# Ranking small steps a constant distance ahead of the text's count, in a two-layer hybrid decoder step

## The chip, the cores and the metric

The kernel runs on one core of one Trainium2 chip. The metric is the device time of one execution in microseconds (us). Three runs of the kernel before took 1163.38, 1163.99 and 1165.86 us; the median is 1163.99.

## The reference

One inference step of a decoder trunk with two layers, for a prompt of 1024 tokens and a sample group of 8 x 8 tokens, 1088 columns in all, with 1024 channels and shared weights. Cut to what matters here, layer 0 is

```
h    = rmsnorm(x) ; proj = h @ w_in                      # 1024 -> 33 tiles of 128 columns
y_a  = a_b * conv3(a_c * a_h) * silu(a_z)                # mixer A
r,k,v,wl,al = token_shift(...)                           # mixer B, RWKV-7, 8 heads of 64
decay = exp(-exp(w_log)) ; kk = normalised k*k_k ; a = sigmoid(...)
S_t  = S_(t-1)*decay_t + (S_(t-1) @ -kk_t) (kk_t*a_t)' + v_t k_t'    # one state per head
y_b  = (groupnorm(S_t r_t) + bonus) * silu(b_z)
x    = x + [y_a, y_b] @ w_out
```

Layer 1 does the same round a pooling mixer and a chunked gating mixer, which are plain dense work. The outputs are the two activations and the new states. All is in 32-bit floats.

## The kernel before

**Dense products.** The 1088 columns are three blocks: block 0 (b0) has the 64 sample columns and 256 of the prompt (320 in all), b1 and b2 have 384 of the prompt each. A product (`product`, L156 to L167) is one 128-wide tile of a projection for one block. Weights and activations are split into a high and a low part, so each of the 8 steps over k is three matmuls (L162, L163, L164), 24 in a product. The weight comes in two halves by DMA (L141); ScalarE makes the high part (L145), VectorE the low part (L146), with four buffers for each (`WB = 4`). The result lies in one of two PSUM buffers, `dn`, until it is evicted. Products form one queue: each is issued after the last matmul of the one before (`later`). Layer 0 has for each block 13 qkv products (`shifted`), 4 gate products (`in_proj_bz`) and 16 of mixer A, and then 8 of the output projection (`out_proj0`) for each block.

**The recurrence.** The state goes in chunks of 64 tokens, and a group is two chunks. Three kinds of small steps serve it, with small matmuls, and short operations on ScalarE (ACT), VectorE (DVE) and GpSimd (POOL):

- `rwkv_prep`, once a group: decays, keys and queries scaled into the tiles BK and AR (L549, L552, L555), the Gram matrices of the chunk (L567, evicted by L570 and written to DRAM by L577).
- `rwkv_inverse`, once a block: it loads the block's Gram matrices again (L611) and inverts their 32 x 32 triangles by 31 steps on DVE, each of two dependent operations (L622, L624), and writes the result to DRAM.
- `recur`, once a block: merges of the inverse (L651, L663), the chain of chunks (`rwkv_chunk`: L772, L774, L791, L793, L797, L807, L808), group norm and output (`group_norm`, `group_out`), and for b0 the sample tokens; between them the preparation of the next block's groups, each behind a finished group of the chain. The steps are traced in streams that may not be queued on PE ahead of given product halves (`marks`, two for each product); the recurrence of b0 and b1 starts 10 marks into the qkv products of the next block, that of b2 at the first product of `out_proj0(b0)`.

The blocks are coupled. The inputs of preparation (`s28`, `tw`, KS, R, V) have one buffer each, so b1's qkv tiles are written over b0's once preparation has read these. The last four input tiles of an output projection are what the recurrence wrote to DRAM (`yr`).

**What sets the order.** Tile queues are fixed when the program is built. A planner plays the program through with its own costs; whenever an engine is free, it takes, of the operations whose inputs it takes to be ready, the one of lowest rank. What isn't ready in that play is passed over. The rank is a running count: each operation traced takes the next number. `tc.high_priority()`, here also `urgent`, sets the count to zero inside its block, and puts it back at the end, so that the operations in the block don't count outside. With a number, the block starts at the count less that number; the result may be negative. Weight splits, evictions, whole qkv products and the recurrence all stand in such blocks, and a qkv product's matmuls have ranks 2 to 25. The count reaches 188 at the preparation of b0, 1361, 1902 and 2398 at the recurrences of b0, b1 and b2, and 5021 at the end. Inside a recurrence block it runs to about 800, and then through the next inverse. The preparation of the sample group and the inverse of b0 are not urgent: they rank by the text.

Of the kernel before, what the change touches and what calls it, by code (L numbers as in the profile page):

```python
# [17 lines left out]
NT = 1088  # L18
AT = (10, 10, 0)
EARLY, RATE, PREP_RATE = 20, 0.7, 0.5  # L20
BLK = ((0, 320), (320, 384), (704, 384))
KAPPA = float(np.exp(-0.5))
RMS_EPS, LN_EPS, GN_EPS = 1e-6, 1e-5, 64e-5
# [50 lines left out]
def build(nc, tc, a):  # L74
# [8 lines left out]
    def mk(p, shape, name, bufs=1, dt=F32):  # L83
        return p.tile(list(shape), dt, name=name, tag=name, bufs=bufs)
# [42 lines left out]
    G.memset(onesc, 1.0)  # L127

    urgent = tc.high_priority
    ydr = {}  # L130
    x1dr = {}

# [308 lines left out]
    def big4(name="iv"):  # L441
        return mk(rw, [128, 32, 32], name, 2)
# [7 lines left out]
    def rwkv_begin(B):  # L450
        n = B.n
        smp = B.i == 0
        s0 = 64 if smp else 0
        B.ng = (n - s0) // 128
        B.gl = ([(0, 64, None)] if smp else []) + [(s0 + 128 * g, 128, g) for g in range(B.ng)]
        B.i0 = 1 if smp else 0
        B.nch = 2 * B.ng + B.i0
        B.PC = mk(rw, [128, 6, 4], "PC", 2)
        B.GT, B.BK, B.AR, B.XT = {}, {}, {}, {}
        B.bon = mk(dr, [128, 4, 384], f"bn{B.i}")  # L460
        B.vd = mk(dr, [384, 512], f"vd{B.i}")
        B.yr = mk(dr, [128, 4, 384], f"yr{B.i}")
        B.dl = mk(dr, [B.nch, 8, 64, 64], f"dl{B.i}")
# [137 lines left out]
    def rwkv_inverse(B):  # L601


        nch, i0 = B.nch, B.i0
        n8 = nch * 8
        Q = 2 * n8
        Lb = big4()
        for (t0, T, g) in B.gl:
            lo, k = (0, 1) if g is None else (i0 + 2 * g, 2)
            for b in range(2):  # L610
                nc.gpsimd.dma_start(Lb[b * n8 + 8 * lo:b * n8 + 8 * (lo + k)],  # L611
                                    B.dl[lo:lo + k, :, 32 * b:32 * b + 32, 32 * b:32 * b + 32].rearrange(
                                        "i h s t -> (i h) s t"))
        X = big4()
        G.memset(X[:Q], 0.0)
        G.memset(X[:Q].rearrange("p a b -> p (a b)")[:, 0:1024:33], 1.0)
        prod = mk(rw, [128, 256], "prod")
        for q in range(31):
            k, r = q + 1, 31 - q
            o = X[:Q, 0:k, k:32]  # L620
            pr = prod[:Q, 0:k * r].rearrange("p (k r) -> p k r", k=k)
            tt(pr, X[:Q, 0:k, q:q + 1].broadcast_to([Q, k, r]),  # L622
               Lb[:Q, q:q + 1, k:32].broadcast_to([Q, k, r]), ALU.mult)
            tt(o, o, pr, ALU.add)  # L624
        for b in range(2):
            nc.gpsimd.dma_start(B.dl[:, :, 32 * b:32 * b + 32, 32 * b:32 * b + 32].rearrange("i h k t -> (i h) k t"),
                                X[b * n8:(b + 1) * n8])
        Xn = big4()
        V.tensor_copy(Xn[:n8], X[:n8].rearrange("p k i -> p i k"))
        B.dn = mk(dr, [nch, 8, 32, 32], f"dn{B.i}")  # L630
        nc.gpsimd.dma_start(B.dn.rearrange("i h k t -> (i h) k t"), Xn[:n8])
# [267 lines left out]
    def out_proj0(B, norms={}):  # L899

        n = B.n
        c0 = BLK[B.i][0]
        h = []
        for k in range(KT):
            x = mk(ev, [128, 384], *(("x", 6) if B.i == 0 else ("ma", 3)))
            nc.sync.dma_start(x[:, :n], ydr[(B.i, k)][:, :n])
            hi = mk(ring, [128, 384], "hi", RB, F32R)
            lo = mk(ring, [128, 384], "lo", RB, F32R)
            split_to(hi[:, :n], lo[:, :n], x[:, :n])
            h.append((hi, lo))  # L910
        acc = None
        for t in range(8):
            if t in norms:
                norm1(norms[t])
            w = weight(a["wout0"][t])
            ps = psum_d(n)
            product(ps, w, h, 0, n)
            if t == 0:
                late_rstd(pd, "dn")
            x = mk(ev, [128, 384], "x", 6)  # L920
            nc.sync.dma_start(x[:, :n], a["xT"][t, :, c0:c0 + n])
            with urgent():
                tt(x[:, :n], ps, x[:, :n], ALU.add)
                if t == 0:
                    acc = mk(cpool, [128, 384], "acc")
                    act(acc[:, :n], x[:, :n], AF.Square)
                else:
                    sq = mk(ev, [128, 384], "d", 1)
                    act(sq[:, :n], x[:, :n], AF.Square)
                    tt(acc[:, :n], acc[:, :n], sq[:, :n], ALU.add)  # L930
            xd = mk(dr, [128, 384], f"xd{B.i}_{t}")
            nc.sync.dma_start(xd[:, :n], x[:, :n])
            x1dr[(B.i, t)] = xd
        late.append((B, acc))
# [12 lines left out]
    for i in range(3):  # L947
        B = Blk()
        B.i, (B.c0, B.n) = i, BLK[i]
        Bs.append(B)  # L950
# [70 lines left out]
    b0, b1, b2 = Bs  # L1021
# [2 lines left out]
        V.tensor_scalar(kkbd[:, p, :], C("bd"), kk2[:, p:p + 1], None, ALU.mult)  # L1024
    rwkv_in(b0)
    rwkv_begin(b0)
    for x in b0.gl:
        with urgent() if x[2] is not None else ExitStack():
            for _ in rwkv_prep(b0, *x):
                pass  # L1030
    rwkv_inverse(b0)
    mark = tc.cur_priority
    rms_stat(b1)
    mixer_a(b0, hs[0], (0,))
# [10 lines left out]
    mixer_a(b1, hs[1], (1, 2))  # L1045
    rms_spread(b2)
    mixer_a(b1, hs[1], (3,))
    with urgent():
        recur(b0, at + AT[0], b1)
        rwkv_inverse(b1)  # L1050
    hs.append(rms_h(b2))
    at = len(marks)
    rwkv_in(b2)
    mixer_a(b2, hs[2], range(4))
    with urgent():
        recur(b1, at + AT[1], b2)
        rwkv_inverse(b2)
    at = len(marks)
    out_proj0(b0)
    out_proj0(b1)  # L1060
    with urgent():
        recur(b2, at + AT[2])
    nc.scalar.dma_start(a["shout"], shout)
    nc.scalar.dma_start(a["cvout"], cvout)
# [328 lines left out]
```

## Time and profile before

| | |
|---|---|
| median of three runs | 1163.99 us |
| profiled execution | 1167.19 us, span 1165.4 us |
| mean granted clock of TensorE over the span | 0.937 |
| PE, DVE, ACT, POOL busy | 1080.9, 741.9, 494.4, 155.9 us |

The profile is of one execution. PE is TensorE, DVE is VectorE, ACT is ScalarE, POOL is GpSimd, and SP issues most DMAs. L162 is line 162 of the kernel. A matmul's recorded duration covers its pipeline, so matmuls overlap in the records, and the step from one start to the next is what one costs. The granted clock is a share of 2.4 GHz.

### The profile page before, as it was taken

The page shows a single profiled execution, that of the slowest core. Times are in us where ns is not written, and L with a number is a line of the kernel's source. Part 1 is how long each engine was busy: PE and PEld are TensorE (multiplying, and loading weights), DVE is VectorE, ACT ScalarE, POOL GpSimd, SP SyncE. Part 2 cuts the span into 40 slices and gives each one's busy share as a digit, 9 for nine tenths or more (in the row PEclk, how much of TensorE's full clock was granted, in tenths as well). Part 3 has the DMA queues.
Part 4 walks back from the last instruction along what each step waited for, and adds up shares of the span by engine and source line. Part 5 has one row for each costly group of instructions (what it writes and reads, how often), then busy time and mean ns, then how long its engine had stood idle before and what let it go on. Part 6 is the DMA issues. An engine that isn't in the chain of part 4 may idle for free. (4 is left out here: it accounts for less than half of the span.)

```text
span 1165.4 us, 21579 instructions
## 1 busy us (share of the span) xinstructions
PE 1080.9 (93%) x8063; PEld 1018.0 (87%) x8063; DVE 741.9 (64%) x1542; ACT 494.4 (42%) x1017; POOL 155.9 (13%) x282
## 2 busy tenths in 40 slices
PE   7999999999998699999979887499999999999996
PEld 6998899898788598988869886399999999999995
DVE  6878885692788766938888743387383344235456
ACT  5376553434655533366654353254311211124232
POOL 2313220201202411102330010000010000000000
PEclk9999999998999799999979886679999999999998
DMA  7464663635345434444468653267311111112345
GB/s 248 154 207 131 160 194 128 200 132 125 99 148 174 123 106 141 139 117 131 133 179 248 211 142 102 58 207 233 109 41 37 39 60 39 37 55 82 111 150 187
DMA packets 135336, 154.83 MB, mean 133 GB/s; under 512 B 45560, under 2 KB 88696, under 8 KB 135232
## 3 DMA queue, kind: packets, MB, share of 16 engines
q1 hardware_dynamic: 130912, 146.36, 41.2%
q0 software_dynamic: 2256, 5.03, 2.1%
q10 hardware_dynamic: 2064, 2.08, 0.6%
q8 instruction: 63, 1.03, 0.4%
q14 instruction: 41, 0.34, 0.1%
HBM read 127.77 MB, written 25.64 MB: 132 GB/s over the span
## 5 line engine op out<-in xcount | busy, mean ns | idle before, releaser
L162 PE MATMUL dn<-hi,whi 128*128 128x384 f32 (+1 forms) x1648 | 553.1, 336 | 28.2 <-ACT q L320 10.6
L163 PE MATMUL dn<-lo,whi 128*128 128x384 f32 (+1 forms) x1648 | 549.6, 333 | 2.9 <-DVE lo L171 2.8
L164 PE MATMUL dn<-hi,wlo 128*128 128x384 f32 (+1 forms) x1648 | 547.2, 332 | 0.0
L162 PEld LDWEIGHTS dn<-hi,whi 128*128 128x128 f32 x1648 | 315.3, 191 | 34.0 <-ACT q L320 11.6
L145 ACT CAST whi<-wraw 128x512 fp32r<-128x512 f32 x326 | 201.4, 619 | 329.6 <-PE dn L163 282.0
L146 DVE TENSOR_TENSOR wlo<-wraw,whi 128x512 fp32r<-128x512 f32 x326 | 223.9, 688 | 161.0 <-ACT whi L145 154.6
L163 PEld LDWEIGHTS dn<-lo,whi 128*128 128x128 f32 x1648 | 315.3, 191 | 8.4 <-DVE lo L171 5.8
L164 PEld LDWEIGHTS dn<-hi,wlo 128*128 128x128 f32 x1648 | 315.2, 191 | 1.5 <-DVE wlo L146 0.5
L807 DVE TENSOR_TENSOR pch<-pch,SV 64x256 f32<-64x256 f32 x32 | 13.9, 434 | 40.6 <-PE pch L797 39.9
L183 POOL TENSOR_TENSOR rms_m<-rms_m,nhalf 128x3 f32<-128x3 f32 (+2 forms) x8 | 6.8, 852 | 216.5 <-DVE rms_m L182 216.5
L567 PE MATMUL pp<-AR,BK 64*128 64x128 f32 x272 | 28.0, 325 | 6.6 <-DVE BK L549 6.6
L567 PEld LDWEIGHTS pp<-AR,BK 64*128 64x128 f32 x272 | 25.3, 226 | 9.2 <-DVE BK L549 5.3
L624 DVE TENSOR_TENSOR iv<-iv,prod 80x31 f32<-80x31 f32 (+23 forms) x93 | 31.2, 336 | 2.1
L622 DVE TENSOR_TENSOR prod<-iv 80x31 f32<-80x31 f32 (+23 forms) x93 | 31.2, 336 | 2.0
L1284 DVE TENSOR_TENSOR big<-dn,x1s 128x384 f32<-128x384 f32 (+1 forms) x24 | 12.8, 535 | 27.6 <-PE dn L164 27.6
L723 POOL TENSOR_TENSOR gvs<-gvs,nhalf 128x8 f32<-128x8 f32 (+1 forms) x9 | 15.8, 1756 | 98.3 <-DVE gvs L722 98.3
L577 POOL DMA_DIRECT2D dl<-GT x32 | 20.2, 634 | 63.8 <-DVE GT L570 62.7
L1290 ACT ACTIVATE sq<-big 128x384 f32<-128x384 f32 (+1 forms) x21 | 10.7, 510 | 35.1 <-DVE big L1284 35.0
L403 POOL COPY pcarry<-up 128x2 f32<-128x2 f32 x12 | 6.4, 530 | 142.2 <-DVE up L394 110.7
L570 DVE TENSOR_TENSOR GT<-pp,cst 128x512 f32<-128x512 f32 x34 | 22.1, 686 | 3.6 <-PE pp L567 3.4
L743 PEld LDWEIGHTS pp<-cst,yc 64*64 64x64 f32 x256 | 12.1, 176 | 13.5 <-DVE yc L724 10.7
L743 PE MATMUL pp<-cst,yc 64*64 64x64 f32 x256 | 14.3, 270 | 10.0 <-DVE yc L724 10.0
(282 smaller groups left out, 1291.4 us busy)
## 6 DMA issues: line engine op xcount, KB each, us to landing
wraw<-win SPq DMA_DIRECT2D x246, 256.0 KB, 2.6
wraw<-wout SPq DMA_DIRECT2D x80, 256.0 KB, 3.2
x<-xT SPq DMA_DIRECT2D x48, 192.0 KB, 3.5
xd<-x SPq DMA_DIRECT2D x16, 192.0 KB, 3.1
xn<-xd SPq DMA_DIRECT2D x16, 192.0 KB, 3.5
x1s<-xd SPq DMA_DIRECT2D x16, 192.0 KB, 2.4
yT<-big SPq DMA_DIRECT2D x16, 192.0 KB, 2.7
i<-vd SPq DMA_DIRECT2D x34, 64.0 KB, 3.4
```

What stands on the lines that cost most here:

```text
L145: A.copy(hi, raw)
L146: tt(lo, raw, hi.bitcast(F32), ALU.subtract)
L162: mm(ps, wh[:, k % 4, :], hh[:, c0:c0 + n], start=k == 0, stop=False)
L163: mm(ps, wh[:, k % 4, :], hl[:, c0:c0 + n], start=False, stop=False)
L164: i = mm(ps, wl[:, k % 4, :], hh[:, c0:c0 + n], start=False, stop=k == KT - 1)
L567: mm(gp[e][:, p * 128:(p + 1) * 128], BK[r, p, c, :, :].rearrange("p a s -> p (a s)"), AR[r, p, c, :, :].rearrange("p a s -> p (a s)"), st ...
L570: tt(GT[:, e::2, :], v3(gp[e]), m[e].unsqueeze(1).broadcast_to([128, 4, 128]), ALU.mult)
L577: nc.gpsimd.dma_start(of_half(B.dl[i], e), GT[64 * e:64 * e + 64, e::2, 0:64])
L622: tt(pr, X[:Q, 0:k, q:q + 1].broadcast_to([Q, k, r]), Lb[:Q, q:q + 1, k:32].broadcast_to([Q, k, r]), ALU.mult)
L624: tt(o, o, pr, ALU.add)
L723: G.tensor_tensor(vs[:T], vs[:T], nhalf[:T], ALU.pow)
L743: mm(ft[r, q:q + 64], yc[r, j:j + 64], ident[r, r], start=True, stop=True)
```

## The change

Four blocks get ranks by `tc.high_priority(6000)`, where they had ranks from zero on, or, for the preparation of b0's sample group and the inverse of b0, by the text. The instructions are the same.

```diff
+AHEAD = 6000
...
     urgent = tc.high_priority
+
+    def ahead():
+
+        return tc.high_priority(AHEAD)
...
     rwkv_begin(b0)
-    for x in b0.gl:
-        with urgent() if x[2] is not None else ExitStack():
+    with ahead():
+        for x in b0.gl:
             for _ in rwkv_prep(b0, *x):
                 pass
-    rwkv_inverse(b0)
+        rwkv_inverse(b0)
...
-    with urgent():
+    with ahead():
         recur(b0, at + AT[0], b1)
         rwkv_inverse(b1)
...
-    with urgent():
+    with ahead():
         recur(b1, at + AT[1], b2)
         rwkv_inverse(b2)
...
-    with urgent():
+    with ahead():
         recur(b2, at + AT[2])
```

## Rows read from the trace of the kernel before

**Rows 1.** The page: busy us of each engine, share of the span, instructions.
```profile
PE 1080.9 (93%) x8063; PEld 1018.0 (87%) x8063; DVE 741.9 (64%) x1542; ACT 494.4 (42%) x1017; POOL 155.9 (13%) x282
```
**Rows 2.** Stretches: from:to length, busy us of PE PEld DVE ACT POOL (instructions), clock, DMA.
```profile
151.00:206.00 55.00, 54.09 (x313) 53.77 (x313) 35.66 (x64) 22.80 (x43) 7.10 (x21) 1.00 0.49 155
206.00:262.00 56.00, 51.10 (x330) 49.49 (x329) 45.92 (x108) 22.69 (x48) 8.50 (x16) 0.97 0.54 167
...
368.00:407.00 39.00, 25.35 (x192) 21.06 (x190) 27.59 (x55) 18.57 (x45) 15.93 (x21) 0.79 0.48 130
...
504.00:588.00 84.00, 83.21 (x1095) 69.05 (x1094) 58.41 (x119) 57.32 (x133) 18.44 (x26) 1.00 0.45 125
588.00:611.00 23.00, 15.20 (x117) 12.34 (x115) 19.04 (x40) 10.91 (x23) 6.77 (x8) 0.70 0.54 159
...
636.00:681.00 45.00, 39.42 (x200) 37.22 (x199) 34.72 (x82) 17.29 (x32) 4.52 (x5) 0.89 0.68 206
681.00:763.00 82.00, 56.28 (x830) 47.21 (x828) 30.52 (x64) 32.46 (x81) 4.93 (x3) 0.63 0.35 93
```
**Rows 3.** PE in order of time, 680 to 757: start, us, instruction, count, wait before.
```profile
680.34 0.34 PE L162 MATMUL dn<-hi,whi 128*128 128x384 f32 x1
...
682.77 0.34 PE L164 MATMUL dn<-hi,wlo 128*128 128x384 f32 x1
...
738.42 0.69 PE L797 MATMUL pch<-i 128*64 128x64 f32 x16
...
756.76 0.69 PE L162 MATMUL dn<-hi,whi 128*128 128x384 f32 x1 [4.38 <-ACT hi L170]
```
**Rows 4.** The same stretches, L162 alone (one third of the dense matmuls).
```profile
151.00:206.00 55.00, 34.99 (x104) 19.39 (x105) 1.00 0.49 155
206.00:262.00 56.00, 26.93 (x77) 14.98 (x77) 0.97 0.54 167
...
368.00:407.00 39.00, 3.10 (x10) 1.67 (x9) 0.79 0.48 130
...
504.00:588.00 84.00, 20.10 (x57) 10.52 (x56) 1.00 0.45 125
588.00:611.00 23.00, 2.73 (x9) 1.65 (x8) 0.70 0.54 159
...
636.00:681.00 45.00, 23.29 (x65) 12.97 (x64) 0.89 0.68 206
681.00:763.00 82.00, 3.62 (x8) 1.76 (x7) 0.63 0.35 93
```
**Rows 5.** DVE in order of time: last BK write of block 0.
```profile
160.79 0.69 DVE L549 TENSOR_TENSOR BK<-tm,iP 64x512 f32<-64x512 f32 x1
```
**Rows 6.** PE in order of time: the Gram matmuls of that group.
```profile
206.76 2.06 PE L567 MATMUL pp<-AR,BK 64*128 64x128 f32 x32
```
**Rows 7.** PE and DVE in order of time: block 0's fourth chunk.
```profile
330.85 0.69 PE L797 MATMUL pch<-i 128*64 128x64 f32 x16
...
358.93 0.42 DVE L807 TENSOR_TENSOR pch<-pch,SV 64x256 f32<-64x256 f32 x1
```
**Rows 8.** DVE in order of time: first qkv tile of block 2.
```profile
395.98 0.62 DVE L339 SCALAR_TENSOR_TENSOR s<-d,pv,q 128x384 f32<-128x384 f32 x1 [0.84 <-PE pp L489]
```
**Rows 9.** DVE groups of the inverses (count, busy, mean ns, idle before); block 2's, timed.
```profile
L624 DVE TENSOR_TENSOR iv<-iv,prod 80x31 f32<-80x31 f32 (+23 forms) x93 | 31.2, 336 | 2.1
L622 DVE TENSOR_TENSOR prod<-iv 80x31 f32<-80x31 f32 (+23 forms) x93 | 31.2, 336 | 2.0
...
638.25 0.55 DVE L171 TENSOR_TENSOR lo<-ma,hi 128x384 fp32r<-128x384 f32 x1
638.72 0.41 DVE L622 TENSOR_TENSOR prod<-iv 96x252 f32<-96x252 f32 x1
```
**Rows 10.** The stretch in which one preparation group ran alone, all engines.
```profile
375.00:394.00 19.00, 12.84 (x95) 10.76 (x95) 13.12 (x27) 9.50 (x22) 6.44 (x11) 0.68 0.48 114
```
**Rows 11.** Waits of SP's queue: us in total, times, longest.
```profile
SPq L674 <- PE py L799: 32.6, 11, 7.5
```

## Prediction

> **What bounds the kernel now.** I read the page first, then the table of stretches, then single lines in time. On the page TensorE (PE) is busy 93% of the span [rows 1], so in the main a product waits for the product before it, and only stretches in which PE is idle, runs at a low granted clock, or runs small steps alone can give anything back. The table of stretches [rows 2] shows where these are: 206 to 262, 368 to 407, 588 to 611, 636 to 681 and 681 to 763. From 504 to 588, where small steps of the recurrence lie between the products, PE is busy 83.21 of 84 us at a granted clock of 1.00.
>
> Two prices come from here. A dense matmul of 384 columns costs PE 0.174 us at full clock: 14 steps of the same sequence from 680.34 to 682.77 [rows 3]; a product has 24, so 4.17 us. A small matmul between products costs 0.059 us: in 504 to 588 there are 1095 instructions [rows 2], 3 x 57 = 171 of them dense [rows 4] (each k has one of L162, L163 and L164), so 84 - 171 x 0.174 = 54.2 us for 924.
>
> What holds the small steps back is seen in three places.
>
> *Behind products of equal rank.* In 151 to 206 PE ran 313 instructions [rows 2], 3 x 104 = 312 of them dense [rows 4]: no small step. Yet the last DVE write of a group's BK was done at 161.48 [rows 5], and the Gram matmuls that read it began at 206.76, all 32 in a row [rows 6]. They had waited 45 us for nothing but their rank. The qkv products stand in an `urgent` block that restarts at zero, so their matmuls rank 2 to 25; the group's Gram step is about the fiftieth of its own block.
>
> *Behind evictions on DVE.* The fourth chunk's state product was on PE from 330.85 to 331.54; the DVE add that reads it ran at 358.93 [rows 7], 27 us late, in a queue filled with work of `urgent` blocks.
>
> *The other way round.* At 395.98 DVE could write the first qkv tile of block 2 (`s28`, one buffer) only when L489 of the last preparation group of block 1 had read it [rows 8]. So late preparation stops the products: that is the hole from 368 to 407.
>
> At the end of this chain stands the exposed tail. The last dense matmul of its run starts at 682.77, the next at 756.76 [rows 3]; between them the whole recurrence of block 2 runs alone, at a granted clock of 0.63 over the stretch [rows 2], a mix of the two levels, 2.4 and 1.2 GHz, while PE idled for 26 of its 82 us.
>
> **The change part by part.** No instruction is added or removed, no wait and no DMA. Four blocks get other ranks: preparation and inverse of block 0 start at 188 - 6000, the recurrence blocks at 1361, 1902 and 2398 less 6000. The text's count ends at 5021, so all four rank ahead of each `urgent` block, which starts at 0, where before their first instructions shared its ranks and the rest came after it.
>
> (a) *b0 preparation and inverse ahead.* The Gram step moves from 206.8 to about 162; the inverse and the first merge follow it, and the recurrence of block 0 starts some 30 to 45 us earlier (30 if the inverse takes longer beside the qkv products). The stretch 206 to 262 has 330 instructions, 231 dense: 40.2 + 99 x 0.059 = 46.0 us of PE work in 56. Gain 10.0 us.
>
> (b) *recurrence of b0 and preparation of b1 ahead.* The hole goes, as preparation is over before block 2's products ask for the buffer. 368 to 407: 192 instructions, 30 dense: 5.2 + 162 x 0.059 = 14.8 us in 39. Gain 24.2 us. Late next is the mark after which the recurrence of block 1 may be queued: 10 marks, so five products, into block 2's qkv, where no chunk of it ran in the trace.
>
> (c) *recurrence of b1, preparation of b2.* 588 to 611: 117 instructions, 27 of them dense, with 320 columns (27 x 0.174 x 320/384 = 3.9), plus 90 x 0.059 = 5.3: 9.2 in 23. Gain 13.8 us.
>
> (d) *recurrence of b2.* It may be queued from the first product of block 0's output projection on. If it starts there, its PE steps lie between the 16 products of two projections. 681 to 763: 830 instructions, 24 dense: 4.2 + 806 x 0.059 = 51.8 in 82. Gain 30.2 us. What stays is the tail behind the last chunk, group norm, output and a round trip through DRAM: 738.42 to 756.76, 18.3 us [rows 3]. It is hidden if the recurrence ends 18 us before the second projection does, bare if not: 0 to 18.3, and I keep 10, about the middle, as six chunks and 16 products are nearly equally long here.
>
> (e) *What pays: evictions and weight splits behind.* On DVE the 62 steps of an inverse take 0.336 us each [rows 9], 20.8 us together, and a preparation group about 13.1 [rows 10]. Dense work bears a DVE delay of two products, 8.4 us, as there are two PSUM buffers and four half-weight buffers. If such a block held DVE whole, an inverse would cost 20.8 - 8.4 = 12.4 us of PE and a group 4.7. But DVE had 55 - 35.66 = 19.3 us free in 151 to 206 [rows 2], and between dependent inverse steps it ran splits that rank far behind them (the L171 at 638.25, rank above 1902, before the L622 at 638.72, rank about 900) [rows 9]. So the bounds are 0 and 3 x 12.4 + 7 x 4.7 = 70 us (three inverses, seven groups that move among products); I take 3 us per inverse, 9 in all, near the lower end because of that row.
>
> (f) *Queues moved past.* On SP the recurrence's loads now go ahead of weight loads. Its chunk loads waited 32.6 us over 11 waits, the longest 7.5 [rows 11]; two products' worth of weights (8.4 us) hide each, and without that cover the price is at most 32.6. I take 0. On POOL the mask stores and inverse loads pass the little carry copies of the qkv tiles; two q buffers hide these.
>
> Sum: 10.0 + 24.2 + 13.8 + 30.2 - 10 - 9 = 59.2 us. The profiled execution took 1167.19 us (span 1165.4), so 1108; the median of the runs is 3.2 lower, so **1105 us**. 636 to 681 has 200 instructions, 195 dense: 33.9 + 0.3 in 45, another 10.8 us which I don't count, as its stall waits for loads that stay.
>
> A rule that speaks against (d): the row shows 924 small matmuls between products at a granted clock of 1.00 [rows 2]. The Trainium skill (Perfetto Trace Analysis, Matmul Optimizations) says that TensorE scales its power with utilization and that matmuls should therefore be issued back to back in batches. If interleaving brought the projections to the 0.63 of the tail, their products, 8 x 4.17 and, with 320 columns, 8 x 3.48 = 61 us, would take 61 x (1/0.63 - 1) = 36 us more, and the time would be about 1141. The trace disagrees, so it gets a chance of 0.04.
>
> **The rivals.**
>
> *PE-bound throughout.* The tail is fully hidden and DVE costs nothing: 78.2 us, 1086, or with the loads of 636 to 681 relieved too 1075. For it: the recurrence moves by more than the stall is long. Against: new order, new waits.
>
> *Only the front.* (a) and (b) come, but the inverse of block 2 stays as slow among the evictions as before and the recurrence still ends behind the projections: 34.2 - 9 = 25, 1139. For it: that inverse's steps already run at 638 [rows 9], over 100 us before dense work resumes, and chunk steps are latencies that rank doesn't shorten.
>
> *Nothing moves.* The order is that of the data and of the marks, 1164. Against it are [rows 5 to 7], where data was there and rank alone held.
>
> *Slower.* DVE becomes the bound where the blocks go: each of ten blocks is planned without gaps, evictions and splits come behind it, PE starves. Price: 70 us, and after each stall a product at the granted clock of 0.63, 4.17 x 0.59 = 2.5 us, so 25 more: 95, against 78.2 - 10 = 68 won; 1191. It decides once a block costs PE more than 68/10 = 6.8 us. For it: 206 to 262 has DVE busy 45.92 of 56 us, and inverses would now meet qkv products. Against: the L171 row.
>
> That the change doesn't do what it says is possible in one respect: block 1's recurrence starts at -4098, while block 0's ends near -3760, so ranks overlap; data keeps the order there, and it costs nothing.
>
> **How the numbers follow.** Forecast 0.50 (1086 to 1125), PE-bound 0.14, front only 0.12, cold clock 0.04, no change 0.06, slower 0.14. The range 1074 to 1150 holds the first four, 0.80. Faster by over 0.2% (2.3 us, about what a measurement of this kernel can tell from no change) 0.80, within it 0.06, slower 0.14.
>
> **What would show it.** (a) The Gram matmuls of block 0's last group run among the first qkv products, not behind the thirteenth. (b) The fourth chunk's L807 follows its L797 within some us, and block 2's first `s28` write waits for no L489. (c) First chunk of block 1 before 450. (d) No stretch of 74 us without dense matmuls; PE idle in the middle falls. (e) Single DVE gaps for evictions between inverse steps; if PE waits on L146 splits in runs of over 7 us during inverses, the slower rival is at work. A recurrence of block 2 that still starts after the second projection would make the forecast wrong.

## Result and profile after

The kernel after takes 1116.83 us (median of 4 runs, 1114.5 to 1121.83), the kernel before beside it 1163.68 (1158.56 to 1165.86). The ratio is 0.9609, with a 95% interval of 0.956 to 0.9658: faster by 47 us. The prediction was 1105, range 1074 to 1150. All code of the change's kernel lies five lines lower than before, so L167 of after is L162 of before, L572 is L567, L812 is L807. The program's instructions are the same, but ACT runs 6 fewer, all of them loads of activation tables (14 where it had 20).

The page of after, busy us of each engine, against [rows 1]:

```profile
PE 1049.7 (94%) x8063; PEld 991.6 (89%) x8063; DVE 735.2 (66%) x1542; ACT 485.3 (44%) x1011; POOL 159.9 (14%) x282
```

The 8063 PE instructions are the same, and yet PE is busy 31.2 us less; its idle time falls from 1165.4 - 1080.9 = 84.5 to 1112.7 - 1049.7 = 63.0 us. These 31.2 + 21.5 are the 52.7 us of the span. The busy part goes with the clock: the mean granted clock is 0.972, where it was 0.937.

Where it went is read from stretches between the same events: start, block 0's first mixer-A product, block 1's first qkv product, block 2's first qkv product, b0's first output product, b2's second output product. Columns as in [rows 2]. Before:

```profile
0.00:75.90 75.90, 67.47 (x442) 65.71 (x442) 58.51 (x130) 39.90 (x76) 17.77 (x59) 0.98 0.66 207
75.90:151.40 75.50, 72.61 (x515) 69.04 (x514) 63.96 (x142) 50.55 (x105) 21.10 (x34) 0.98 0.54 155
151.40:351.70 200.30, 193.71 (x1506) 175.32 (x1505) 135.94 (x274) 93.83 (x197) 25.65 (x49) 0.97 0.48 145
351.70:588.30 236.60, 220.10 (x1936) 200.44 (x1936) 173.34 (x355) 121.80 (x262) 55.28 (x84) 0.95 0.47 135
588.30:764.00 175.70, 136.60 (x1315) 122.40 (x1314) 105.76 (x237) 73.40 (x157) 16.01 (x16) 0.75 0.53 154
```

After:

```profile
0.00:97.50 97.50, 83.99 (x557) 78.17 (x558) 72.47 (x170) 51.83 (x109) 24.60 (x73) 0.96 0.52 164
97.50:184.20 86.70, 75.11 (x506) 71.26 (x505) 74.42 (x183) 42.17 (x89) 26.21 (x31) 0.94 0.58 163
184.20:396.90 212.70, 199.90 (x1601) 181.15 (x1601) 161.35 (x330) 104.61 (x219) 40.58 (x67) 0.96 0.50 148
396.90:604.50 207.60, 199.99 (x1807) 184.54 (x1806) 150.33 (x311) 109.27 (x231) 41.56 (x66) 0.97 0.50 143
604.50:709.90 105.40, 100.83 (x1240) 92.45 (x1239) 70.00 (x138) 62.48 (x138) 7.46 (x5) 1.00 0.73 222
```

The stretches change by +21.6, +11.2, +12.4, -29.0 and -70.3 us; what lies behind them is 401.4 us before and 402.8 after. So the front is **45.2 us longer** and the back **99.3 shorter**. Some of it is only moved: up to block 2's first qkv product PE runs 557 + 506 + 1601 = 2664 instructions where it ran 2463, nearly all of the difference small steps; at 0.059 us each about 12 us of work. That leaves a loss of some 33 us in front and a gain of some 87 behind.

**The front.** The longest stall of PE in the second stretch, from the list of waits (us in total, times, longest):

```profile
PE dn L184 <- DVE acc L284: 7.0, 1, 7.0
```

The matmuls on both sides of it, PE in order of time:

```profile
119.01 0.31 PE L169 MATMUL dn<-hi,wlo 128*128 128x320 f32 x1
126.35 1.44 PE L184 MATMUL dn<-onesc,acc 128*128 128x1 f32 x6 [7.04 <-DVE acc L284]
```

L284 sums the squares of block 1's input for its norm and ranks by the text; the product queue stands until the last of these sums. The input had landed by 78.0 us, and before, the last sum was done at 74. The last squares stand on ACT behind weight splits (L150) that wait for their loads, ACT in order of time:

```profile
119.04 0.62 ACT L150 CAST whi<-wraw 128x512 fp32r<-128x512 f32 x1 [2.02 <-DMA wraw<-win]
120.44 0.62 ACT L150 CAST whi<-wraw 128x512 fp32r<-128x512 f32 x1 [0.78 <-DMA wraw<-win]
120.96 0.52 ACT L283 ACTIVATE d<-x 128x384 f32<-128x384 f32 x1
123.34 0.62 ACT L150 CAST whi<-wraw 128x512 fp32r<-128x512 f32 x1 [1.86 <-DMA wraw<-win]
123.86 0.52 ACT L283 ACTIVATE d<-x 128x384 f32<-128x384 f32 x1
```

So rank left the sums until late, and weight loads that came late held the last of them. The clock falls within the stall and stays low behind it, as these two stretches show (columns as above):

```profile
118.00:126.00 8.00, 1.31 (x9) 1.05 (x8) 4.47 (x9) 3.23 (x6) 0.16 (x1) 0.77 0.92 268
126.00:130.00 4.00, 3.65 (x15) 3.65 (x16) 1.81 (x9) 0.00 (x0) 0.88 (x1) 0.50 0.60 203
```

Two more waits of PE in the front are of small steps ranked ahead, whose own input isn't there yet when PE's queue comes to them:

```profile
PE pp L572 <- DVE BK L554: 8.5, 3, 5.0
PE pp L601 <- DVE V L344: 5.6, 2, 5.4
```

Before, the first of these came to 1.1 us in the front and the second doesn't stand there.

**The small steps.** Single lines in order of time, which answer to [rows 5 to 8]: block 0's last BK write and its Gram matmuls, the fourth chunk's state product and its add, block 2's first qkv tile:

```profile
106.73 0.69 DVE L554 TENSOR_TENSOR BK<-tm,iP 64x512 f32<-64x512 f32 x1
106.24 3.28 PE L572 MATMUL pp<-AR,BK 64*128 64x128 f32 x32 [0.47 <-DVE BK L554]
...
265.70 0.69 PE L802 MATMUL pch<-i 128*64 128x64 f32 x16
276.14 0.42 DVE L812 TENSOR_TENSOR pch<-pch,SV 64x256 f32<-64x256 f32 x1
...
404.76 0.61 DVE L344 SCALAR_TENSOR_TENSOR s<-d,pv,q 128x384 f32<-128x384 f32 x1
```

The Gram matmuls follow their input at once, where they had waited 45 us. The add is still 10 us late, where it was 27. The qkv tile waits for nothing.

**The tail.** PE in order of time: the last chunk's state product (738.42 in [rows 3]), the last group output, and the output projection that needs it:

```profile
672.85 0.69 PE L802 MATMUL pch<-i 128*64 128x64 f32 x16
...
682.46 1.15 PE L748 MATMUL pp<-cst,yc 64*64 64x64 f32 x32
...
706.25 0.44 PE L167 MATMUL dn<-hi,whi 128*128 128x384 f32 x1 [1.11 <-ACT hi L175]
```

The recurrence of block 2 now begins at 610.2, where it was 686.9, and its 832 small steps lie among the products of 604.5 to 709.9 at a clock of 1.00.

### The profile page after: what moved, and what is told of

Read it like the earlier page. It is cut to its first block, busy times and chain, and to the rows that moved or that the text cites. A ratio compares the mean times of both kernels' runs of the same rounds, so it can differ in the third digit from the quotient of the medians.

```text
span 1112.7 us, 21507 instructions
## 1 busy us (share of the span) xinstructions
PE 1049.7 (94%) x8063; PEld 991.6 (89%) x8063; DVE 735.2 (66%) x1542; ACT 485.3 (44%) x1011; POOL 159.9 (14%) x282
## 4 chain that ended last, share of the span: by engine, by line
PE 75%; DVE 12%; DMA 5%; ACT 3%; issue 2%; POOL 1%; SPq 0%; DVEq 0%; ACTq 0%
PE dn L167 21%; PE dn L168 20%; PE dn L169 20%; DVE wlo L151 2%; DMA wraw<-win 2%; PE pp L572 1%; DMA xn<-xd 1%; DVE BK L554 1%; ACT whi L150 1%; PE pch L777 1%; PE pl L1182 1%; PE pl L1247 1%; PE pch L796 1%; DVE GT L575 1%; DVE prod L627 1%
## 5 line engine op out<-in xcount | busy, mean ns | idle before, releaser
L167 PE MATMUL dn<-hi,whi 128*128 128x384 f32 (+1 forms) x1648 | 554.3, 336 | 12.3 <-ACT whi L150 7.1
L150 ACT CAST whi<-wraw 128x512 fp32r<-128x512 f32 x326 | 200.2, 619 | 318.9 <-PE dn L168 277.5
L167 PEld LDWEIGHTS dn<-hi,whi 128*128 128x128 f32 x1648 | 313.6, 190 | 20.7 <-ACT whi L150 9.3
L572 PE MATMUL pp<-AR,BK 64*128 64x128 f32 x272 | 28.5, 317 | 9.5 <-DVE BK L554 8.5
L572 PEld LDWEIGHTS pp<-AR,BK 64*128 64x128 f32 x272 | 25.5, 216 | 12.9 <-issue 6.9
L331 DVE TENSOR_TENSOR d<-q 128x384 f32<-128x384 f32 (+1 forms) x39 | 20.7, 530 | 6.0 <-ACT q L325 4.5
L1203 ACT ACTIVATE big<-dn 128x384 f32<-128x384 f32 (+1 forms) x12 | 5.7, 472 | 35.0 <-PE dn L169 35.0
L928 DVE TENSOR_TENSOR x<-dn,x 128x384 f32<-128x384 f32 (+1 forms) x24 | 12.8, 532 | 10.6 <-PE dn L169 6.9
```

The costliest lines, as they stand in the source:

```text
L150: A.copy(hi, raw)
L167: mm(ps, wh[:, k % 4, :], hh[:, c0:c0 + n], start=k == 0, stop=False)
L331: tt(d[:, :n], q[:, 0:n], q[:, 1:1 + n], ALU.subtract)
L572: mm(gp[e][:, p * 128:(p + 1) * 128], BK[r, p, c, :, :].rearrange("p a s -> p (a s)"), AR[r, p, c, :, :].rearrange("p a s -> p (a s)"), st ...
```

## Experiments

Times are medians; ratios are formed from the single runs against the kernel before on the same chip, with 95% intervals, so they differ a little from quotients of medians. Its medians there were 1165.28 us (7 runs) beside the first four kernels, 1163.35 beside the next four, 1165.36 beside the last four.

**Is it the order among the blocks, or being ahead at all?** e3 lets each block start at -6000:

```diff
-        return tc.high_priority(AHEAD)
+        return tc.high_priority(tc.cur_priority + AHEAD)
```

> The changed kernel, but each of the four blocks starts at the same rank, -6000, instead of a constant distance ahead of the text. If what counts is that the blocks rank ahead of the urgent products and evictions, the time is that of the changed kernel, within 0.5%. If what counts is that the blocks keep their order among themselves, most of the gain is lost: 1140 to 1165 us.

1119.07 us, 0.9599 (0.9568 to 0.963). PE's queue is the change's own. That the blocks keep their order among each other does nothing; that they rank ahead of the `urgent` blocks does.

**Each part alone.** e1 is the change with block 0's part put back; e2 has that part alone.

```diff
 # e1
-    with ahead():
-        for x in b0.gl:
+    for x in b0.gl:
+        with urgent() if x[2] is not None else ExitStack():
...
-        rwkv_inverse(b0)
+    rwkv_inverse(b0)
```

> The changed kernel with one part undone: preparation and inverse of block 0 rank as before; the three recurrence blocks stay 6000 ahead. Theory A (the chain of the recurrence sets the end, and block 0's early start buys about what it costs on VectorE): the first merge is near 280 us again instead of 207, the front up to block 2's first qkv product is 20 to 35 us shorter than in the changed kernel (there 397), but the recurrence of block 2 starts well after block 0's output projection, so that the second projection's end is followed by a stall; 1105 to 1130 us against 1117. Theory B (block 0's part is cost alone, as the recurrence of block 1 waited for its mark in any case): the front is shorter and nothing is given back, 1085 to 1095.

> The kernel before with one part alone: only preparation and inverse of block 0 rank 6000 ahead; the recurrence blocks start at zero as before. Theory A: block 0's recurrence starts early (first merge near 207 us), but the preparation of block 1 still waits behind qkv products of equal rank, and the tail of block 2 stays exposed: 1150 to 1185 us, so little of the gain of 47. Theory B: cost alone, 1185 to 1200.

e1: 1121.82 us, 0.9596 (0.9538 to 0.9654; its longest run, 1130.83, is left out of the ratio), the same as the change. Its first stretches are 149.1 us long, not 184.2, but the next one takes up 28 of these 35 us, so block 2's first qkv product comes 7 us earlier where 20 to 35 were expected (columns as above; start to b1's first qkv product, and on to b2's):

```profile
0.00:149.10 149.10, 136.93 (x955) 132.09 (x956) 122.34 (x272) 90.27 (x179) 38.05 (x93) 1.00 0.61 184
149.10:389.90 240.80, 219.96 (x1706) 196.10 (x1706) 172.13 (x350) 110.78 (x241) 44.37 (x74) 0.94 0.49 139
```

e2: 1136.07 us, 0.9753 (0.9718 to 0.9789), a larger gain than expected. Its hole is gone too. Its theory A, by which block 1's preparation would still wait, fell. The parts don't add: each alone brings that preparation forward.

e9 has the block of b0's recurrence with b1's preparation and inverse alone ahead, e10 the two later blocks alone:

```diff
 # e9, the kernel before with
-    with urgent():
+    with ahead():
         recur(b0, at + AT[0], b1)
         rwkv_inverse(b1)
 # e10, the kernel before with the same edit at recur(b1, ...) and recur(b2, ...)
```

> The kernel before with one block ahead: block 0's recurrence, which contains block 1's preparation, and block 1's inverse. Theory C, formed after the qkv products' rank turned out not to be needed: what decides is whether block 1's preparation ends before block 2's first qkv product, since it is then not caught behind that block's 13 products, and they don't wait for its buffers. Here it ends before (about 380 against 390), so nearly the whole gain comes: 1115 to 1135 us. Rival (each block's rank brings its own part of the gain): 1140 to 1155.

> The kernel before with the other two blocks ahead: the recurrences of blocks 1 and 2, with block 2's preparation and inverse. Theory C: block 1's preparation is caught as before, the hole at 368 to 407 stays; block 2's recurrence starts at most some 20 us earlier: 1140 to 1163 us. Rival (the gain is in passing evictions late, where the tail was): 1115 to 1130.

e9: 1135.72 us, 0.973 (0.9676 to 0.9784), just over what was expected, 30 of the 47 us. e10: 1150.74 us, 0.9878 (0.9835 to 0.9921), as expected. What parts them is whether block 1's last Gram eviction (L571 here) comes before block 2's first qkv product. In order of time, e9:

```profile
388.22 1.28 DVE L571 TENSOR_TENSOR GT<-pp,cst 128x512 f32<-128x512 f32 x2
397.04 0.34 PE L163 MATMUL dn<-hi,whi 128*128 128x384 f32 x1
```

e10, the same lines in order of time:

```profile
351.28 0.34 PE L163 MATMUL dn<-hi,whi 128*128 128x384 f32 x1
444.00 2.48 DVE L571 TENSOR_TENSOR GT<-pp,cst 128x512 f32<-128x512 f32 x4
```

and e10's stretch from that product to behind that eviction, columns as above:

```profile
351.30:448.40 97.10, 81.40 (x531) 75.64 (x529) 70.17 (x132) 42.96 (x92) 26.07 (x44) 0.89 0.46 131
```

In e10 the product queue stood for 28.8 us before block 2's fifth qkv product, in the kernel before for 28.9; in no other kernel here does it stand there.

**Is it TensorE's rank against the qkv products?** e4 is the kernel before with only the matmuls of these products at the text's rank; e5 is the change with them ahead of everything.

```diff
 # e4: weight, PSUM buffer and token shift stay in `urgent`, the matmuls leave it
-        q, d = shift_tile(B, j, h)
+            w = weight(a["win0"][16 + j])
+            ps = psum_d(B.n)
+        product(ps, w, h, 0, B.n)
+        with urgent():
+            q, d = shift_tile(B, j, ps)
 # e5: the change, and the same with
+        with tc.high_priority(tc.cur_priority + 20000):
+            product(ps, w, h, 0, B.n)
```

> The kernel before with one edit: the matmuls of the qkv products rank by the text instead of 2 to 25; their weight loads, splits and evictions stay urgent, and so do the recurrence blocks, which start at zero. If TensorE's rank against the qkv products was what held the small steps back, preparation no longer waits for the thirteenth product, the hole before block 2's fifth product goes, and most of the gain comes without any other change: 1110 to 1135 us. If the rank on VectorE and ScalarE against evictions and splits was what held them, little changes: 1150 to 1165.

> The changed kernel with one edit: the matmuls of the qkv products rank at -20000, so they again outrank the small steps on TensorE, as in the kernel before; on VectorE, ScalarE and the queues the four blocks stay ahead of everything. Theory (TensorE's rank against the qkv products is what held the small steps): preparation waits for the thirteenth product again, the tail of block 2 is exposed, and the cost at the front stays: 1150 to 1190 us. Rival (the rank on VectorE and ScalarE brings the gain): still 1110 to 1130.

e4: 1096.41 us, 0.9432 (0.9371 to 0.9492): one edit, without any block ahead, and it beats the change. e5: 1121.49 us, 0.9632 (0.9586 to 0.9678): the gain stays, where the theory that TensorE's rank alone decides wanted 1150 to 1190. That theory fell. TensorE's hold was still there: among b1's thirteen qkv products (180.4 to 234.6) e5 ran 317 instructions, 312 of them dense, where the change ran 943 (184.2 to 279.9). The small steps' rank on the other engines is enough by itself for most of the gain, and so is the products' rank on PE.

**Do the two add?** e6 is e4 with the three recurrences ahead, e7 is e4 with b0's part ahead:

```diff
 # e6: the change + e4's edit, b0's part as before (as in e1)
 # e7: the kernel before + e4's edit + b0's part in `with ahead():`
```

> The qkv products' matmuls at text rank (the edit that alone gave 1096) and, beside it, the three recurrence blocks 6000 ahead; block 0's preparation and inverse as before. Being ahead on VectorE and ScalarE is all that the constant adds here. Theory: it adds nothing or costs a little, 1090 to 1115. Rival (chain steps gain by passing evictions): 1070 to 1088.

> The qkv products' matmuls at text rank and, beside it, block 0's preparation and inverse 6000 ahead; the recurrence blocks start at zero. Theory: the front up to block 0's first mixer product takes 20 us more, as it did in the changed kernel, and an earlier start of the recurrence gives little back: 1105 to 1125 against 1096. Rival (an earlier recurrence pays): under 1090.

e6: 1103.33 us, 0.9465 (0.9429 to 0.9501). e7: 1107.6 us, 0.9522 (0.9498 to 0.9546). Neither adds anything to e4; b0's part costs it about 11 us.

**What does the front pay for?** e8 is the change with evictions, token shifts and weight splits ahead of the small steps, and e4's edit; e11 is e8 with b0's part as before; e12 is the change with b0's inverse alone put back to the text's rank.

```diff
 # e8 (and e11), besides e4's edit
-    urgent = tc.high_priority
+    urgent = lambda: tc.high_priority(tc.cur_priority + 20000)
...
-            with tc.high_priority():      # weight split
+            with urgent():
 # e12
     with ahead():
         for x in b0.gl:
             for _ in rwkv_prep(b0, *x):
                 pass
-        rwkv_inverse(b0)
+    rwkv_inverse(b0)
```

> The changed kernel, with all that is urgent (evictions, weight splits, weight loads of the qkv products) ranked at -20000, before the four blocks, and the qkv products' matmuls at text rank, behind the blocks as in the changed kernel. If the cost at the front is that evictions and splits stand behind the small steps on VectorE and ScalarE, it goes: 1085 to 1105. If it is TensorE's own order, the small steps that cut into block 0's first products, the time stays at 1112 to 1125.

> Evictions and splits before the small steps, qkv products' matmuls at text rank, the three recurrence blocks 6000 ahead, and block 0's preparation and inverse as in the kernel before. It leaves out both costs that the runs so far show at the front: the early start of block 0 (about 25 us up to block 1's first qkv product) and evictions standing behind small steps. If the two add up and the recurrence is still early enough: 1080 to 1095 us. If the later start of the recurrence gives back what the front wins, as with block 0's part undone alone: 1096 to 1110.

> The changed kernel with block 0's inverse alone back at its text rank; its preparation stays ahead. If the inverse on VectorE is what costs at the front, the stretch from block 0's first mixer product to block 1's first qkv product falls from 87 us to about 75, and the whole to 1100 to 1112. If it is the preparation's steps that cut in earlier, that stretch stays within 3 us of 87, and the whole at 1113 to 1125.

e8: 1102.06 us, 0.9485 (0.9441 to 0.9529). Its front up to block 1's first qkv product is 168.3 us, between the change's 184.2 and the 151.4 of before, with nearly as many PE instructions (1029; 1063 in the change):

```profile
0.00:168.30 168.30, 150.35 (x1029) 142.53 (x1030) 137.13 (x318) 93.54 (x185) 42.49 (x100) 0.97 0.56 175
```

e7, which has e4's edit and b0's part ahead but not the evictions and splits, takes 184.1 us to that point, as the change does. So about half of the cost up to there is evictions and splits behind small steps. Up to block 2's first qkv product e8 keeps 12 of these 16 us (384.9; 396.9 in the change). e11: 1097.41 us, 0.9419 (0.9375 to 0.9462), which ties with e4: the second of its forecasts. e12: 1112.4 us, 0.9554 (0.9507 to 0.96), between its two forecasts. Its two stretches that answer to the change's second and third:

```profile
100.50:177.60 77.10, 69.20 (x469) 67.31 (x468) 67.88 (x160) 37.39 (x72) 13.14 (x25) 0.96 0.58 169
177.60:397.70 220.10, 207.10 (x1633) 186.05 (x1632) 167.84 (x352) 107.63 (x234) 45.77 (x70) 0.95 0.50 146
```

The first is 9.6 us shorter than the change's, the second 7.4 longer: the inverse isn't what the front pays for, or it pays wherever it lies; as intervals overlap, this run settles no more. The wait for L284, in all traces:

```
kernel                                                  PE (dn) waits for acc of b1
before, e1, e4, e6, e9, e10, e11 (b0's part as before)   none
change, e2, e3, e5, e7, e12 (prep ahead)                7.0  7.6  5.7  5.2  6.4  5.9 us
e8 (prep ahead, urgent work further ahead)              none
```

It comes with the preparation of b0 ahead, not with its inverse (e12 has it), and leaves when urgent work goes further ahead. The late weight loads go with it: between 110 and 130 us ACT waits 3.6 to 5.3 us for them in each of the six kernels with the stall, and in none of the eight others. No run parts the two, nor shows what made the loads late.

## Why the prediction was right

The table has event times of nine of the traces, on which the cause rests (us; the hole is the stand of the product queue before block 2's fifth qkv product).

```
         b1's last Gram  b2's first   hole   b2's last  first chunk  start of b2's
         eviction        qkv product         eviction   of b2        2nd output product
before   446.0           351.7        28.9   605.3      686.9        764.0
e10      445.8           351.3        28.8   594.7      682.3        753.9
change   327.7           396.9        none   534.6      610.2        709.9
e1       381.7           389.9        none   543.9      612.9        718.6
e2       358.5           392.1        none   554.0      625.4        731.3
e4       365.5           375.9        none   533.3      604.1        703.6
e5       338.6           394.2        none   551.0      617.5        722.1
e9       388.8           397.0        none   556.1      630.7        725.5
e11      369.1           379.5        none   535.2      605.4        691.7
```

What all gains above 2% share is the order of the first two columns: block 1's preparation is done before block 2's qkv products begin. Where it isn't, its last group is caught behind the thirteenth of these (in the kernel before this one ends at 442.5), they wait for its single buffers, and everything of block 2 follows some 40 to 80 us later. Five kernels that the table leaves out (e3, e6, e7, e8, e12) have the same order, and e9 and e10, which split the change's recurrence blocks between them, fall on either side of it. No run moved one of the two columns alone. That was the step of the prediction called "the other way round" [rows 8]. The prediction named two holds ahead of it, rank on TensorE [rows 5 and 6] and evictions on DVE [rows 7]; e4 lifts the first alone; e5 keeps it and lifts the second, with the rank on the other engines and queues; and either is enough for most of the gain.

- **(b) The hole, 24.2 us: right.** The fourth stretch is 29.0 us shorter, of which 129 instructions fewer make about 7.6, and the qkv tile at 404.76 waits for nothing. (The first chunk of b1 is at 425.0, not 506.9.)
- **(c) and (d), 13.8 + 30.2 - 10: right in kind, too small.** The back gains 87 us where these and (b) made 58. The prediction kept 10 us of the tail, as it made the recurrence end with the second projection; it ends about 15 before (its last output at 687, the projection at about 702), so the tail is hidden: in the product that needs it only the wait of 1.11 us for a split is left. And it left out the 10.8 us of 636 to 681, whose stall it held to come from loads that stay. No such wait is left in the change: PE is busy 41.65 of the 42.7 us of that projection (659.8 to 702.5), at a clock of 1.00. The time at half clock in 681 to 764 went as well.
- **(a), +10 us, and (e), -9 us: wrong, the mis-sized terms.** Together +1, measured about -33. Of the 45.2 us that the front is longer, PE's idle time in the first three stretches is 37.9 - 17.9 = 20 and 12 is moved work. The other 13 is more busy time: length times granted clock over these stretches leaves some 18 us lost to the clock in the change and 9 before, so the lower clock is at most about 9 of the 13, and the rest isn't traced. Nearly all of the 20 us of idle time is three waits: L184's 7.0, and those of L572 and L601 (8.5 - 1.1 and 5.6). (a) placed the Gram step at 162; ranked ahead of all it ran at 106, the preparation took its place from the products, and the mixer starts 21.6 us later. (e) priced inverses on DVE. These alternated with one dense operation per step, as expected, DVE in order of time within block 0's inverse:

```profile
146.02 0.41 DVE L627 TENSOR_TENSOR prod<-iv 80x255 f32<-80x255 f32 x1
146.35 0.27 DVE L415 SCALAR_TENSOR_TENSOR ma<-us,pv,ma 128x64 f32<-128x64 f32 x1
146.55 0.41 DVE L629 TENSOR_TENSOR iv<-iv,prod 80x255 f32<-80x255 f32 x1
146.88 0.48 DVE L421 TENSOR_TENSOR ma<-ma,xt 128x320 f32<-128x320 f32 x1
```

What it missed is text-ranked work that the products need, the L284 sums (a stall of 7.04 us and half clock behind it), and small steps that stand at the head of PE's queue before their input is there. These two errors and the undercounted back had opposite signs: 33 lost instead of 1 won, 87 won instead of 58. That the sum came so close is in part luck: its terms were off by 34 and 29 us and nearly cancelled. In the profiled executions the forecast was a gain of 59.2 us and 52.7 came: 34 - 29 = 5 us are these two, 1.4 the end behind the last stretch. By the medians 47 came: the profiled run of before lies 3.5 us above the median beside the change, that of the change 2.3 below its own.
- **(f) Queues, 0: right for the waits that it priced, too small elsewhere.** SP's waits for the chunks' products, against [rows 11], fell:

```profile
SPq L679 <- PE py L804: 13.5, 9, 2.5
```

But ACT waits 4.7 us for weight loads inside the L284 stall, and none there before; the prediction held that two products' worth of weights hide such delays.

- **The slower rival** did not come, because the planner kept the gaps, as the L171 row of [rows 9] had said. Its mechanism is real at a smaller size: e8 got 16 us of the front back by ranking evictions and splits first. **PE-bound throughout** had the back right (the tail hidden, 636 to 681 relieved), but not that the front costs nothing. **Only the front** came out the other way round: the front lost and the back won.
- **The cold clock** did not come in the change: 604.5 to 709.9 stands at 1.00 with 832 small steps among its products. The Trainium skill (Perfetto Trace Analysis, Matmul Optimizations) wants matmuls back to back in batches, since power follows utilization. PE is busy 100.83 of 105.40 us here, so that does not speak against this stretch, nor against the prediction's row (83.21 of 84 us): small matmuls between the products took nothing from the clock. e4's profiled execution shows the other side (from 604 to 628; columns as above):

```profile
604.00:628.00 24.00, 24.00 (x325) 19.46 (x326) 2.70 (x6) 12.79 (x34) 0.00 (x0) 0.50 0.24 60
```

PE had idled 1.05 us up to 601.57; the clock stood at half from about 604 on, with PE busy in every us, small steps between products. What brought it down isn't shown: the change has a wait of 1.05 us too, up to 665.68, and its clock stayed at 1.00. At full clock the same work would by estimate have taken some 12 us less (half of 24.00), and e4's other three runs took 1094.27 to 1097.38 us where this one took 1109.23. So the 0.04 of that rival was not empty.

**What stays open.** e2 gains 2.5% though only b0's part moves, and e9 2.7%, and both lack the change's full gain; which later waits make the difference was not taken apart. Of the front's 33 us, the three waits of PE and e8's 16 us are shown (they overlap, as L284's stall is gone in e8); what made PE's busy time longer isn't. That e4 and e11 tie at 1096 and 1097 suggests a common bound; no run tried to pass it.

## What to carry to other kernels

Where two blocks share single buffers, look whether the consumer of the first finishes before the producer of the second begins: here every kernel with that order gained about 2.5% or more, and the one changed kernel without it, e10, 1.2%. A block ranked ahead of everything takes its place from everything, from text-ranked work that the products need too; price the stretch that receives the work, not only the one that it leaves. And try the smaller edit: taking the qkv products' matmuls out of their urgent rank gave 1096, the four blocks ahead 1117.

## What the runs showed of the hardware

The span times the mean granted clock hardly differs between these kernels: 1165.4 x 0.937 = 1092 before, 1112.7 x 0.972 = 1082 in the change, 1107.1 x 0.976 = 1081 in e4's profiled execution and 1092.1 x 0.991 = 1082 in its shortest. The product is the time that the span would take at the full clock if every part of it went with the clock. By it 42 of the 52.7 us between before and after are time at the lower clock. That is too much, as idle time doesn't go with the clock: PE's busy time fell by 31.2 us for the same matmuls, its idle time by 21.5. Nearly all of e4's spread between its runs is such time by the same product, 1081 against 1082. And a stall of TensorE cost more than its length here: 7.04 us up to 126.35, and a clock of 0.50 from 126 to 130 under PE work.
